# Weight chunks subtracted in quarters, and attention weights scaled by one operation with two per-row factors

## The chip, the cores and the metric

The kernel runs on one core of one Trainium2 chip. The metric is the time of one execution in microseconds on the device. The core has five engines that run side by side, each through its own queue in order: TensorE (PE in the profile, PEld for its weight loads), VectorE (DVE), ScalarE (ACT), GpSimd (POOL) and SyncE (SP), which here issues the DMAs. Tiles lie in SBUF, and matmuls write into eight PSUM banks.

## The reference, cut to what matters

One layer of a decoder trunk over 1024 tokens of width 1024, in float32: a normalisation, one input projection, a convolution group, a group of sparse attention with three gated branches, an output projection with a residual add, then a second normalisation and a SwiGLU feed-forward part.

```python
def hybrid_layer(x, ...):
    h = rms_norm(x, attn_norm)
    z = h @ w_in
...
    conv_out = conv_mixer(a_conv, conv_w, conv_b, conv_ln_g, conv_ln_b)
...
    gates = jax.nn.sigmoid(g).reshape(b, t, N_KV_HEADS, Q_PER_KV, N_BRANCH)
    nsa_out = nsa_attention(q, kc, vc, ks, vs, kw, vw, gates)
    x = x + concatenate([conv_out, nsa_out]) @ w_out
    h = rms_norm(x, ffn_norm)
    gate, up = jnp.split(h @ w_gate_up, 2, axis=-1)
    return x + (jax.nn.silu(gate) * up) @ w_down
```

Inside the attention, each branch is a masked softmax `p = exp(s - m) / max(sum, 1e-30)`, multiplied with the values, and the branch outputs are added with the gates as weights: `gb[..., 1:2] * o_s + gb[..., 2:3] * o_w`. So a row of `exp(s - m)` has two factors that are constant along the row: the gate and the inverse of the row's sum.

## The kernel before, in words

Matmuls are made as three products each. A float32 matrix is split into a high part, its rounding to the matmul's format, and a low part, the rest; high x high, low x high and high x low are summed in PSUM. For activations the split is the helper `split` (ACT copies L194, DVE subtracts L195). For weights it is `load_w`: SP loads a chunk of 128 x 1024 numbers (1096 for the value weights) into `w_raw`, ACT rounds it into `w_hi` (L189), and POOL subtracts into `w_lo` (L190). There are 168 such chunks on POOL, and eight more, for the compression weights, that DVE subtracts. Two buffers hold raw chunks and three hold each part; a `Feed` asks for chunks some places ahead. A second loader, `out_loads_k`, does the same with 16 chunks of 512 columns for the output projection of the second half (L887, L888).

The program has stages. In the first (until about 250 us) x is normalised and transposed, the compressed branch is made, the first half's rows are projected, and DVE runs the convolution: `conv_taps` adds 31 taps, each a `scalar_tensor_tensor` over 128 x 512 (L481), whose two tensor inputs both lie in SBUF. From about 250 us the function `attention` runs, woven by hand (`weave`, with costs and ratios) with a second stream that fills PE: first the second half's projections and the first half's output projection, from about 600 us passes of the feed-forward part for the first half (`ffn`, matmuls L991 and L1011). In the later attention part the taps of the second half run too (`slow`), now with factors that POOL copies into `c2` (L477, L478). From about 1000 us the second half's output projection and the rest of the feed-forward part follow.

An attention step is one of 64 pairs of a query tile and a branch, with three heads each. `scores` makes the scores on PE (L677 to L681); DVE adds the distance penalty and finds the minimum (L685); ACT takes the exponential with the row's sum in `l3` (L688). After the third head DVE bounds `l3` from below (L693), takes the reciprocal (L695) and multiplies it by the gates into `cf` (L696), all on 128 x 3 numbers. POOL then multiplies each head's row tile `pr` by its column of `cf`, spread along the row (L702): three operations of 128 to 1024 columns a step, 192 in all. `transposed` brings `pr` through PE (L708) and splits it, `product` multiplies with the values (L725, L726). Scores are asked for at least two steps ahead of their products, further where buffers and `LEAD` allow.

In `ffn`, ACT and DVE form `silu(gate) * up` in `af` (L998) and `split` turns it into `aw`; its subtraction (L195, `aw<-af,aw`) reads two SBUF tiles, while the other splits by DVE mostly read one PSUM and one SBUF tile.

The order of each engine's queue is not that of the source: the kernel is built with a scheduler that simulates the engines (`schedule_with_timeline_sim=True`) and places the instructions by that, except in the very last pass, where PE is kept in source order.

Of the kernel before, what the change touches and what calls it, by code (L numbers as in the profile page):

```python
# [11 lines left out]
F32 = mybir.dt.float32  # L12
F32R = mybir.dt.float32r
AF = mybir.ActivationFunctionType
ALU = mybir.AluOpType
# [3 lines left out]
P = 128  # L19
# [8 lines left out]
REP = HEADS // GROUPS  # L28
# [45 lines left out]
TICK = 5.0  # L74
SLOW0 = 36
PACE_B = 4
PRE_DVE = 0, 0
ACCS = "zs"
ACCS2 = "z"
ACCS3 = "z"  # L80
PACE_C = 0


@with_exitstack
def tile_hymba(ctx: ExitStack, tc, x, attn_norm, w_in, conv_w, conv_b, conv_ln_g, conv_ln_b,
# [3 lines left out]
    dve, act, pool, pe, sp = nc.vector, nc.scalar, nc.gpsimd, nc.tensor, nc.sync  # L89
# [12 lines left out]
    def bank(name, tag="z"):  # L102
        return ps.tile([P, 512], F32, tag=tag, name=name, bufs=BANKS[tag])
# [22 lines left out]
    gates = cp.tile([P, NT, 36], F32, name="gates")  # L126
# [51 lines left out]
    def load_w(parts, a, b, eng=pool):  # L178
        raw = wp.tile([P, WCH], F32, tag="raw", name="w_raw", bufs=2)
        hi = wp.tile([P, WCH], F32R, tag="whi", name="w_hi")  # L180
        lo = wp.tile([P, WCH], F32R, tag="wlo", name="w_lo")
        back = PACE_B if phase[0] == 0 else PACE_C
        if len(pace) >= back > 0:
            pool.tensor_copy(raw[:, 0:1], pace[-back][:, 0:1])
        n = a * b
        v = raw[:, :n].rearrange("p (k c) -> p k c", k=a)
        for c, src in parts:
            sp.dma_start(v[:, :, c:c + src.shape[-1]], src.rearrange("(k p) c -> p k c", p=P))
        act.copy(hi[:, :n], raw[:, :n])  # L189
        eng.tensor_sub(lo[:, :n], raw[:, :n], hi[:, :n].bitcast(F32))  # L190
        return (hi[:, :n].rearrange("p (k c) -> p k c", k=a), lo[:, :n].rearrange("p (k c) -> p k c", k=a))

    def split(hi, lo, src):
# [43 lines left out]
    def win_chunk(c0):  # L237
        return load_w([(0, w_in[0, :, c0:c0 + P])], KT, P)

    xts = []  # L240
    for t in range(NT):
# [4 lines left out]
        else:  # L246
            q_, tag = (p2, "xt") if t < 7 else (py, "y")
# [165 lines left out]
    def value_loads(c0, g0):  # L413
        return [lambda kh=kh: load_w([(0, w_in[0, kh * 512:(kh + 1) * 512, c0:c0 + 256]),
                                      (256, w_in[0, kh * 512:(kh + 1) * 512, C_G + g0:C_G + g0 + 18])], 4, 274)
                for kh in range(2)]
# [182 lines left out]
    def attention(p, bufs, extra, ratio):  # L599
# [4 lines left out]
        def size(st):  # L604
            i = st[2]
            return i + 1 if st[3] == 0 else min(i + 1, 5)
# [44 lines left out]
        def scores(st, r):  # L651
            part, g, i, br = st
            hf = i // 4
            if r == 0:
                load(st)
            nk = size(st)
            k0 = i + 1 - nk
            n = nk * P
            cut = {5: 384, 7: 384}.get(nk, 512)
            edges = [0, n] if n <= 512 else [0, cut, n]  # L660
            if r == 0:
                prs[st] = [p.tile([P, REP], F32, tag="l3", name="l3", bufs=26)]
            l3 = prs[st][0]
            q2, kk_ = q2s[g, i], kt[part, g, br]
            if hf:
                pr = p.tile([P, T], F32, tag="pr", name="pr", bufs=bufs["pr"])
            else:
                if br == 1:
                    both[g, i, r] = p.tile([P, T], F32, tag="pr", name="pr", bufs=bufs["pr"])
                pr = both[g, i, r][:, (1 - br) * 512:(2 - br) * 512]  # L670
            m = 3.0e38
            dur = 0.0
            for a, e in zip(edges, edges[1:]):
                s = bank("s", "s")
                sv = s[:, :e - a]
                kk = slice(k0 * P + a, k0 * P + e)
                pe.matmul(sv, q2[:, 0, r, :], kk_[:, 0, kk], start=True, stop=False)  # L677
                if br == 0 and hf:
                    pe.matmul(sv, q2[0:80, 1, r, :], kk_[0:80, 1, kk], start=False, stop=True)
                else:  # L680
                    pe.matmul(sv, q2[:, 0, r, :], kk_[:, 1, kk], start=False, stop=True)  # L681
                dur += 2 * max(0.107, (e - a) / 2400.0)
                mn = p.tile([P, 1], F32, tag="m", name="m", bufs=16)
                t0 = T if br and nk == 5 and a == 0 else T - n + a
                dve.tensor_tensor_reduce(pr[:, a:e], sv, base[:, t0:t0 + e - a], SLOPES[g * REP + r], m,  # L685
                                         ALU.add, ALU.min, mn)
                m = mn
            act.activation(pr[:, :n], pr[:, :n], AF.Exp, bias=m, scale=-1.0, accum_out=l3[:, r:r + 1])  # L688
            prs[st].append(pr)
            if r == REP - 1:  # L690
                pace.append(l3)
                cf = p.tile([P, REP], F32, tag="cf", name="cf", bufs=10)
                dve.tensor_scalar(l3, l3, 1e-30, None, op0=ALU.max)  # L693
                gv = gates[:, i, g * 9:(g + 1) * 9].rearrange("p (r b) -> p r b", b=3)[:, :, 1 + br]
                dve.reciprocal(l3, l3)  # L695
                dve.tensor_tensor(cf, gv, l3, op=ALU.mult)  # L696
                for r2 in range(REP):
                    x_ = prs[st][1 + r2][:, :n]
                    if r2 < PRE_DVE[part]:
                        dve.tensor_scalar(x_, x_, cf[:, r2:r2 + 1], None, op0=ALU.mult)  # L700
                    else:
                        pool.tensor_tensor(x_, x_, cf[:, r2:r2 + 1].to_broadcast([P, n]), op=ALU.mult)  # L702
            return dur

        def transposed(st, kk):
# [45 lines left out]
        for n in range(-1, len(steps)):  # L751
            phase[:] = [steps[max(n, 0)][0], n]
            want, ahead = n + 2, 0.0
            while want < len(steps) and fits(n, want) and ahead < LEAD:
                ahead += cost[want - 1]
                want += 1
            want = min(want, len(steps))
            todo = [(st, r) for st in steps[asked:want] for r in range(REP)]
            asked = max(asked, want)
            if n < 0:  # L760
                load_pct(steps[0])
            elif steps[n][3] and n + 2 < len(steps):
                load_pct(steps[n + 2])
            ts = range(size(steps[n])) if n >= 0 else []
            m = max(len(ts), 1)
            total, given = len(todo), 0
            for k in range(m):
                if n >= 0:
                    ph, pl = transposed(steps[n], k)
                    yield 0.33  # L770
                    pend.append((steps[n], k, ph, pl))
                    if len(pend) > LAG:
                        yield product(*pend.pop(0))
                while given * m < total * (k + 1):
                    yield scores(*todo[given])
                    given += 1
            for fn in extra.get(n, ()):
                d = fn()
                if d:
                    yield d  # L780
# [100 lines left out]
    def out_loads_k(p):  # L881
        def load(kt, ch):
            raw = p.tile([P, 512], F32, tag="oraw", name="o_raw")
            hi = p.tile([P, 512], F32R, tag="ohi", name="o_hi", bufs=2)
            lo = p.tile([P, 512], F32R, tag="olo", name="o_lo", bufs=2)
            sp.dma_start(raw, w_out[0, kt * P:(kt + 1) * P, ch * 512:(ch + 1) * 512])
            act.copy(hi, raw)  # L887
            pool.tensor_sub(lo, raw, hi.bitcast(F32))  # L888
            return hi, lo
        return [lambda kt=kq * 4 + k, ch=ch: load(kt, ch) for kq in range(2) for ch in range(2) for k in range(4)]  # L890

# [241 lines left out]
```

## Time and profile before

| | us |
|---|---|
| median of 3 runs | 1563.87 |
| lowest and highest | 1562.23, 1564.19 |
| profiled execution, its own time | 1562.75 |
| its span in the trace | 1561.0 |
| mean granted TensorE clock | 0.979 |

In the profile, a group's row gives line, engine, operation and tiles, then shapes and count, busy microseconds and mean nanoseconds of one, and last the idle time of the engine ahead of it with what ended it. A row of one line or tile gives shortest/median/longest nanoseconds. A row of the timeline gives start, length, engine and operation, with followers of one kind merged (x3). The chain of waits is followed back from the last instruction, at each step to what released it.

### The profile page before, as it was taken

To read this page: it belongs to the slowest core of one execution; us is meant where nothing else is said; L and a number is where in the kernel's file an instruction comes from. 1 tells how busy PE (TensorE), PEld (TensorE's weight loads), DVE (VectorE), ACT (ScalarE), POOL (GpSimd) and SP (SyncE) were. 2 spreads that over 40 slices of the span, in tenths; PEclk is the share of its full clock that TensorE was granted. 3 is DMA by queue.
4 is the path that set the end of the run, shared out by engine and by line. 5 is a ranking of instruction groups with operands and counts; after the bars stand their busy time and mean duration, and the time that the engine had idled before them with its cause. 6 is when DMAs were issued, how large, how long until landed. Compare 5 with 4: busy or idle time off the path is not lost.

```text
span 1561.0 us, 21253 instructions
## 1 busy us (share of the span) xinstructions
PE 1475.6 (95%) x7271; PEld 1227.0 (79%) x7271; DVE 920.2 (59%) x1998; ACT 717.0 (46%) x1464; POOL 771.2 (49%) x618
## 2 busy tenths in 40 slices
PE   6998999899889989989999999999999999999997
PEld 5877978787668768878888887778788888888876
DVE  7596563778777677887778877332532432222333
ACT  6334564668576566555665564322311222222223
POOL 6253253767556546656656655444322243444443
PEclk9999999999989999999999999999999999999999
DMA  6254566566476463234245222742121233233332
GB/s 195 79 144 133 169 192 213 170 179 189 132 255 173 118 142 87 70 100 117 68 119 135 60 61 74 242 145 88 48 75 54 89 114 94 81 107 96 94 95 81
DMA packets 224265, 190.44 MB, mean 122 GB/s; under 512 B 15400, under 2 KB 193420, under 8 KB 224156
## 3 DMA queue, kind: packets, MB, share of 16 engines
q1 hardware_dynamic: 224156, 189.07, 41.3%
q8 instruction: 58, 0.95, 0.3%
q14 instruction: 51, 0.42, 0.1%
HBM read 155.27 MB, written 33.75 MB: 121 GB/s over the span
## 4 chain that ended last, share of the span: by engine, by line
PE 69%; DVE 12%; ACT 6%; DMA 5%; issue 4%; POOL 2%; SPq 1%; POOLq 0%; DVEq 0%; ACTq 0%
PE gu L991 28%; PE dn L1011 14%; PE pt L708 4%; DVE cacc L481 4%; PE vo L427 3%; PE wo L934 3%; PE wo L952 3%; PE o L726 2%; PE o L725 2%; PE s L677 2%; PE zc L314 2%; DMA w_raw<-in_w_in_dram 2%; DMA mix<-mix_d 2%; PE zo L314 2%; ACT w_hi L189 1%
## 5 line engine op out<-in xcount | busy, mean ns | idle before, releaser
L190 POOL TENSOR_TENSOR w_lo<-w_raw,w_hi 128x1024 fp32r<-128x1024 f32 (+1 forms) x168 | 419.2, 2502 | 436.8 <-ACT w_hi L189 413.6
L991 PE MATMUL gu<-h,w_hi 128*128 128x512 f32 x1408 | 455.0, 396 | 0.6 <-DVE x L1016 0.6
L189 ACT CAST w_hi<-w_raw 128x1024 fp32r<-128x1024 f32 (+1 forms) x176 | 183.9, 1051 | 353.8 <-PE gu L991 180.8
L991 PEld LDWEIGHTS gu<-h,w_hi 128*128 128x128 f32 x1408 | 263.3, 188 | 57.6 <-DVE x L1016 1.1
L991 PE MATMUL gu<-h,w_lo 128*128 128x512 f32 x704 | 278.3, 395 | 0.0
L1011 PE MATMUL dn<-w_hi,aw 128*128 128x512 f32 x704 | 235.8, 399 | 12.7 <-DVE aw L195 6.0
L702 POOL TENSOR_TENSOR pr<-pr,cf 128x640 f32<-128x640 f32 (+5 forms) x192 | 214.4, 1144 | 66.3 <-DVE cf L696 51.9
L688 ACT ACTIVATE pr<-pr,m 128x640 f32<-128x640 f32 (+5 forms) x192 | 141.5, 738 | 121.4 <-DVE m L685 116.6
L998 DVE TENSOR_TENSOR af<-gu,af 128x512 f32<-128x512 f32 x44 | 30.3, 688 | 246.0 <-PE gu L991 184.9
L1011 PEld LDWEIGHTS dn<-w_hi,aw 128*128 128x128 f32 x704 | 131.4, 188 | 48.8 <-DVE aw L195 8.9
L195 DVE TENSOR_TENSOR pl<-pt,ph 128x384 fp32r<-128x384 f32 x264 | 140.5, 550 | 42.6 <-ACT ph L194 41.0
L1016 DVE TENSOR_TENSOR x<-dn,x 128x512 f32<-128x512 f32 x176 | 114.8, 684 | 76.0 <-PE dn L1011 75.8
L991 PEld LDWEIGHTS gu<-h,w_lo 128*128 128x128 f32 x704 | 132.3, 188 | 28.9
L194 ACT CAST ph<-pt 128x384 fp32r<-128x384 f32 x264 | 118.2, 478 | 72.3 <-PE pt L708 55.8
L708 PE MATMUL pt<-ident,pr 128*128 128x128 f32 x792 | 141.5, 279 | 6.7 <-DVE pl L195 5.7
L1011 PE MATMUL dn<-w_lo,aw 128*128 128x512 f32 x352 | 138.8, 394 | 0.0
L708 PEld LDWEIGHTS pt<-ident,pr 128*128 128x128 f32 x792 | 103.8, 143 | 24.9 <-DVE pl L195 4.0
L685 DVE CUSTOM_DVE_ANT_0 pr<-s,base 128x384 f32<-128x384 f32 (+3 forms) x192 | 101.3, 533 | 27.1 <-PE s L681 15.6
L677 PE MATMUL s<-kt,q 128*128 128x384 f32 (+3 forms) x288 | 104.2, 363 | 11.5 <-DVE m L685 8.0
L314 PE MATMUL zo<-h,w_hi 128*128 128x512 f32 x320 | 107.0, 407 | 5.4 <-ACT w_hi L189 2.8
L725 PE MATMUL o<-ph,vt 128*128 128x384 f32 x264 | 101.9, 386 | 4.0 <-ACT ph L194 3.8
L726 PE MATMUL o<-pl,vt 128*128 128x384 f32 x264 | 94.2, 357 | 2.4 <-DVE pl L195 2.4
(208 smaller groups left out, 2454.0 us busy)
## 6 DMA issues: line engine op xcount, KB each, us to landing
w_raw<-in_w_gate_up_dram SPq DMA_DIRECT2D x80, 512.0 KB, 3.8
w_raw<-in_w_in_dram SPq DMA_DIRECT2D x40, 512.0 KB, 4.2
w_raw<-in_w_down_dram SPq DMA_DIRECT2D x40, 512.0 KB, 3.3
mix<-mix_d SPq DMA_DIRECT2D x8, 1024.0 KB, 7.8
q<-q_d SPq DMA_DIRECT2D x80, 96.0 KB, 2.7
qc<-q_d SPq DMA_DIRECT2D x32, 192.0 KB, 3.6
pc_d<-pct SPq DMA_DIRECT2D x16, 384.0 KB, 3.1
pct<-pc_d SPq DMA_DIRECT2D x32, 192.0 KB, 3.8
```

The source lines that it names most:

```text
L189: act.copy(hi[:, :n], raw[:, :n])
L190: eng.tensor_sub(lo[:, :n], raw[:, :n], hi[:, :n].bitcast(F32))
L195: dve.tensor_sub(lo, src, hi.bitcast(F32))
L314: pe.matmul(o, a[:, k, :], b[hf][k // 4][:, k % 4, :], start=n == 0, stop=n == 3 * KT - 1)
L677: pe.matmul(sv, q2[:, 0, r, :], kk_[:, 0, kk], start=True, stop=False)
L688: act.activation(pr[:, :n], pr[:, :n], AF.Exp, bias=m, scale=-1.0, accum_out=l3[:, r:r + 1])
L702: pool.tensor_tensor(x_, x_, cf[:, r2:r2 + 1].to_broadcast([P, n]), op=ALU.mult)
L708: pe.transpose(pt[:, r * P:(r + 1) * P], prs[st][1 + r][:, kk * P:(kk + 1) * P], ident)
L725: pe.matmul(o[:, :384], v, ph, start=False, stop=False)
L726: pe.matmul(o[:, :384], v, pl, start=False, stop=last)
L991: pe.matmul(o, w[:, k, :], h2[si][h][k // 4][:, k % 4, :], start=n == 0, stop=n == 3 * KT - 1)
L1011: pe.matmul(o, aws[si][:, a, k, t * P:(t + 1) * P], b[:, 0, ch * 512:(ch + 1) * 512], start=n == 0, stop=n == 5)
```

## The change

POOL's subtraction of a weight chunk becomes four subtractions of a quarter of the columns each, and the one of the second loader two halves. DVE no longer forms `cf`, and POOL multiplies each row tile by two per-row factors in one tensor-scalar operation: the inverse sum in `l3` and the gate, read from `gates` itself. The constant `PRE_DVE`, which was zero for both parts, goes with the branch that used it.

```diff
-PRE_DVE = 0, 0
...
+PIECES = 4
...
@@ load_w
         act.copy(hi[:, :n], raw[:, :n])
-        eng.tensor_sub(lo[:, :n], raw[:, :n], hi[:, :n].bitcast(F32))
+        step = n // PIECES if eng is pool else n
+        for c in range(0, n, step):
+            q = slice(c, c + step)
+            eng.tensor_sub(lo[:, q], raw[:, q], hi[:, q].bitcast(F32))
...
@@ scores
                 pace.append(l3)
-                cf = p.tile([P, REP], F32, tag="cf", name="cf", bufs=10)
                 dve.tensor_scalar(l3, l3, 1e-30, None, op0=ALU.max)
-                gv = gates[:, i, g * 9:(g + 1) * 9].rearrange("p (r b) -> p r b", b=3)[:, :, 1 + br]
                 dve.reciprocal(l3, l3)
-                dve.tensor_tensor(cf, gv, l3, op=ALU.mult)
+
                 for r2 in range(REP):
                     x_ = prs[st][1 + r2][:, :n]
-                    if r2 < PRE_DVE[part]:
-                        dve.tensor_scalar(x_, x_, cf[:, r2:r2 + 1], None, op0=ALU.mult)
-                    else:
-                        pool.tensor_tensor(x_, x_, cf[:, r2:r2 + 1].to_broadcast([P, n]), op=ALU.mult)
+                    c = g * 9 + r2 * 3 + 1 + br
+                    pool.tensor_scalar(x_, x_, l3[:, r2:r2 + 1], gates[:, i, c:c + 1], op0=ALU.mult, op1=ALU.mult)
...
@@ out_loads_k
             act.copy(hi, raw)
-            pool.tensor_sub(lo, raw, hi.bitcast(F32))
+            for c in (0, 256):
+                q = slice(c, c + 256)
+                pool.tensor_sub(lo[:, q], raw[:, q], hi[:, q].bitcast(F32))
             return hi, lo
```

In the built program the instructions are otherwise the same, with two more loads of an ACT table; the scheduler moves many of them by some places. POOL's four quarters of a chunk stand mostly in a row, and PE waits for them one by one: 390 products with a `w_lo` wait for POOL, where 119 did.

## The prediction

> **What bounds the kernel now.** I read the page first, then the busy time by stage, then the chain of waits.
>
> ```profile
> span 1561.0 us, 21253 instructions
> PE 1475.6 (95%) x7271; PEld 1227.0 (79%) x7271; DVE 920.2 (59%) x1998; ACT 717.0 (46%) x1464; POOL 771.2 (49%) x618
> ...
> PE 69%; DVE 12%; ACT 6%; DMA 5%; issue 4%; POOL 2%; SPq 1%; POOLq 0%; DVEq 0%; ACTq 0%
> ```
> ```profile
> 0.00:250.00 250.00, 222.01 (x1170) 190.28 (x1171) 165.61 (x305) 121.56 (x274) 107.74 (x110) 0.96 0.54 161
> 250.00:600.00 350.00, 317.10 (x1721) 269.51 (x1720) 258.75 (x800) 223.78 (x582) 207.74 (x221) 0.95 0.57 163
> 600.00:1000.00 400.00, 387.88 (x2009) 324.81 (x2008) 310.42 (x662) 232.61 (x417) 238.14 (x183) 1.00 0.36 100
> 1000.00:1500.00 500.00, 496.69 (x2157) 401.44 (x2156) 161.97 (x198) 120.81 (x160) 192.44 (x92) 1.00 0.30 94
> ...
> 1184.41 44.55 PE gu L991 x192
> ```
> The columns are the stretch, its length, busy PE, weight loads, DVE, ACT, POOL, then clock, DMA share and GB/s; the last row, of the chain in order of time, is 192 matmuls without a break, 0.232 us apart. TensorE sets the time. From 1000 to 1500 us it is busy for 496.7 of 500 us, so nothing done to POOL or DVE can pay there. What can be won lies before 1000 us, where PE idles 28, 33 and 12 us (a busy PE there isn't at its peak either), and on the chain the largest share that isn't PE is DVE's, 12%. POOL is idle half the time and holds 2% of the chain. Its own speed matters little, but what it does to DVE matters:
>
> ```profile
> L195 DVE TENSOR_TENSOR aw<-af,aw x44: 677/2210/2877, 611.6 to 1542.4; 128x512 fp32r<-128x512 f32 x44
> ...
> L481 DVE SCALAR_TENSOR_TENSOR cacc<-y,c,cacc x58: 735/1134/2860, 589.9 to 955.9; 128x512 f32<-128x512 f32 x58
> ...
> 85.78 2.82 POOL L190 TENSOR_TENSOR w_lo<-w_raw,w_hi 128x1024 fp32r<-128x1024 f32 x1
> ...
> 83.61 2.76 DVE L481 SCALAR_TENSOR_TENSOR cacc<-y,cols,cacc 128x512 f32<-128x512 f32 x1
> 86.29 0.14 DVE L372 COPY bc<-h 128x1 f32<-128x1 f32 x1
> ```
> The first two rows give shortest/median/longest ns of DVE operations with both inputs in SBUF. An `aw` takes 677 ns at best but 2210 in the median; the excess never passes 2.2 us, about one POOL subtraction. The last rows show it once: a tap that needs 735 ns stands for 2.76 us, until POOL's subtraction ends at 85.8 us. The next subtraction, begun at 85.78, takes 2.82 us. Such an operation and a POOL instruction exclude each other, and a waiting DVE operation gets in between two POOL instructions.
>
> **Quartering, from 600 to 1000 us.**
>
> ```profile
> 600.00:1000.00 400.00, 25.42 (x14) 1.00 0.36 100
> ...
> 600.00:1000.00 400.00, 70.95 (x56) 1.00 0.36 100
> ...
> 600.00:1000.00 400.00, 0.00 (x0) 99.45 (x41) 1.00 0.36 100
> ...
> 600.00:1000.00 400.00, 111.07 (x71) 1.00 0.36 100
> ...
> by line: PE gu L991 26.9%; PE dn L1011 15.9%; PE pt L708 8.7%; issue 5.4%; DVE cacc L481 5.1%; PE o L726 4.9%; PE o L725 4.7%; PE s L677 4.1%; DVE aw L195 3.8%; DVE pr L685 2.7%; DVE pl L195 2.4%; PE s L679 2.3%; ACT w_hi L189 1.7%; PE s L6
> ...
> PE dn L1011 <- DVE aw L195: 6.0, 5, 2.9
> ```
> The four windows are `aw`, the taps L481, POOL's subtractions L190 (DVE's zero ahead of them) and its scalings L702; a number in brackets is a count. An `aw` averages 25.42/14 = 1.82 us, 63% of it over the 0.677 floor; a tap 70.95/56 = 1.27 us, 42% over 0.735. The chain holds 3.8% of 400 = 15.2 us of `aw` and 5.1% = 20.4 us of taps, so the blocked part on it is 0.63 x 15.2 + 0.42 x 20.4 = 18.1 us.
>
> How much goes? A random arrival waits half the POOL instruction that it meets: (99.45 x 1.21 + 111.07 x 0.78)/400 = 0.52 us now. Prices of the new pieces:
>
> ```profile
> L190 POOL TENSOR_TENSOR w_lo<-w_raw,w_hi 128x1024 fp32r<-128x1024 f32 x160 | 398.7, 2499 | 415.8 <-ACT w_hi L189 392.7 <-DVE cm L538 9.7 <-issue 8.9
> L702 POOL TENSOR_TENSOR pr<-pr,cf 128x640 f32<-128x640 f32 x60 | 82.6, 1404 | 16.9 <-DVE cf L696 13.5 <-PE s L677 3.2
> L888 POOL TENSOR_TENSOR o_lo<-o_raw,o_hi 128x512 fp32r<-128x512 f32 x16 | 20.7, 1293 | 42.4 <-ACT o_hi L887 42.4
> ...
> L281 POOL TENSOR_SCALAR cb<-cb 128x512 f32<-128x512 f32 x1 | 2.1, 2066 | 0.1
> ...
> L302 POOL TENSOR_SCALAR_AFFINE_SELECT base<-base 128x1024 f32<-128x1024 f32 x1 | 1.0, 1034 | 0.0
> L282 POOL TENSOR_SCALAR_AFFINE_SELECT cb<-cb 128x512 f32<-128x512 f32 x1 | 0.6, 648 | 0.0
> ```
> A subtraction of 512 costs 1293 ns and one of 1024 costs 2499, so the fixed part is 2 x 1293 - 2499 = 87 ns and a quarter is 87 + 2412/4 = 690 ns. The new scaling has no good row. Its nearest kin by pattern, one input and one output, are the selects: 648 ns at 512 and 1034 at 1024, which puts 640 columns at 745 ns, 0.53 of the 1404 now. The one tensor-scalar row takes 2066 ns for 512, which scaled is 2.58 us, 1.84 times. But that row stood against DVE:
>
> ```profile
> 23.93 2.07 POOL L281 TENSOR_SCALAR cb<-cb 128x512 f32<-128x512 f32 x1
> ...
> 23.36 4.09 DVE L203 SCALAR_TENSOR_TENSOR xt<-xt,rs,grow 128x1024 f32<-128x1024 f32 x3
> ...
> L203 DVE SCALAR_TENSOR_TENSOR rows<-x,rs,rows x12: 1270/1284/3447, 569.1 to 1246.0; 128x1024 f32<-128x1024 f32 x12
> ```
> Three two-input operations of 1.27 us each at best fill 23.36 to 27.45 us with 0.28 us lost. Had POOL needed the port for 2 us, they would have lost 2. Most of that span was waiting, so I take 0.53. [...]
>
> With quarters of 0.69 us and scalings of 0.83 (0.53 x 1.56) the mean wait becomes (41 x 4 x 0.69 x 0.345 + 71 x 0.83 x 0.415)/400 = 0.16 us: 69% goes, 12.5 of the 18.1 us. A second chain lies behind, so not all is time. PE itself waited for `aw` 6.0 us, of which 69% is 4.1. Between 4.1 and 12.5 I take **-8 us**.
>
> **The attention stage, 250 to 600 us.**
>
> ```profile
> L693 DVE TENSOR_SCALAR l<-l x64: 146/169/2335, 254.2 to 942.0; 128x3 f32<-128x3 f32 x64
> ...
> L693 DVE TENSOR_SCALAR l<-l 128x3 f32<-128x3 f32 x64 | 28.0, 438 | 21.1 <-ACT pr L688 20.8
> ...
> L696 DVE TENSOR_TENSOR cf<-gates,l 128x3 f32<-128x3 f32 x64 | 17.0, 266 | 1.2
> ```
> The product `cf` (L696) goes, 17.0 us of DVE. L693 averages 0.438 us over a floor of 0.146, so 64 x 0.29 = 18.6 us are blocked there. With the product that is 36 us at most, over both attention parts. A step's three scalings also end 3 x 0.66 = 2 us earlier. But scores are asked for steps ahead, and what covers the chain from scores to scaling now keeps covering it. Between 0 and 0.69 x 18.6 + 17.0 = 30 us I take a tenth, **-3 us**.
>
> **The first stage, and what the change adds.**
>
> ```profile
> L481 DVE SCALAR_TENSOR_TENSOR cacc<-y,cols,cacc 128x512 f32<-128x512 f32 x62 | 59.4, 994 | 0.6
> ...
> by line: DVE cacc L481 14.6%; PE zc L314 12.5%; PE vo L427 9.6%; issue 7.2%; POOL w_lo L190 5.1%; ACT w_hi L189 3.5%; DMA w_raw<-in_w_in_dram 3.4%; ACT cs L544 3.2%; PE tp L210 2.5%; DVE w_lo L190 2.5%; DMA xt<-in_x_dram 2.4%; DMA w_raw<-in
> ...
> 113.77 4.05 DVE L481 SCALAR_TENSOR_TENSOR cacc<-y,cols,cacc 128x512 f32<-128x512 f32 x6
> ...
> 114.86 5.23 POOL L190 TENSOR_TENSOR w_lo<-w_raw,w_hi 128x1024 fp32r<-128x1024 f32 x1 [5.54 <-ACT w_hi L189]
> ```
> Taps hold 14.6% of 250 = 36.5 us of the chain, 26% of it over 735 ns, so up to 0.69 x 9.5 = 6.6 us could go. Against it, the port works the other way too: at 114.86 us a subtraction sat behind six taps in a row and took 5.23 us instead of 2.4. A chunk needs one gap in such a run now and four after. I set this stage at **0**, between -6.6 and the price of the third rival.
>
> POOL pays 3 x 87 = 261 ns more per chunk, 168 chunks, 44 us. It hides under POOL's 51% idle; at the end a chunk is wanted once in 24 matmuls (5.6 us at 0.232 us each). Were the cover gone, the 5.1% of 250 us with L190 on the chain, about five chunks, would pay 1.3 us. The product by a low part can now start at its first quarter, up to 1.8 us sooner for those five, 9 us at most. I take **0** for both. Extra PE waits on met semaphores and local shuffles of the built order I take at nothing: PE at 496.7 of 500 us covers them late, and early they are inside the range.
>
> **Sum.** -8 - 3 + 0 = -11 us on the profiled execution's own 1562.75 us (its span and 1.75 us around it): 1551.8. The median shown, 1563.87, lies 1.1 us above it, so 1553 us.
>
> **Rivals.** *Hidden anyway.* DVE's lost time sits beside waits for DMA and ACT (11% of the chain), and what is won is waited again before the saturated stage. Then 1561 to 1567. For it: only 6.0 us of PE idle names `aw`. Against: 18 us of blocking on the chain itself. *It doesn't do what it says*: DVE finds no gap between quarters in a row. The same time, about 1565; the tap let in at 85.8 speaks against it. *DVE starves POOL* in runs of taps before 130 us: each further quarter sits through a run, 5.23 - 2.4 = 2.8 us, three times a chunk, 8.5 us. It decides if three of the first stage's chunks are late enough to hold PE: +25 us against the 11, so about 1577. For it: 114.86. Against: the taps too are finite, and the projections' own DVE work, which waits for PE, breaks their runs. [...] *The slow scaling*: at 1.84 times, POOL has 0.84 x 111 = 93 us more in the 400 us from 600 on, 331 of 400 busy, and a step's three scalings end 3.5 us later; if a third of 64 steps show it, +75 us, 1638.
>
> **How the numbers follow.** Forecast 0.57 (1536 to 1560, the bounds of the terms), hidden 0.08, not as said 0.03, starving 0.22, slow scaling 0.10. The range 1535 to 1577 holds the first four but for tails and leaves the last out. No change is within 0.2%, 3.1 us, what a measurement of this kernel can tell. Faster 0.57, same 0.11, slower 0.32.
>
> **What would show it.** In the new profile: `aw`'s median below 1.3 us; taps' means near 0.8 us; scalings of 640 near 0.75 us; quarters near 0.69 us; L693 near 0.2 us; DVE's share of the chain under 12%; 1000 to 1500 us unchanged. It is wrong if subtractions in the first stage take 3 us a quarter with PE waiting for L190, or if scalings take over 1.4 us.

## The result, and the profile after

The changed kernel takes 1524.01 us (median of 4 runs, 1521.04 to 1528.14), against 1563.05 us (4 runs, 1559.24 to 1564.19) of the kernel before: ratio 0.976, 95% interval 0.9736 to 0.9784. It is 39 us faster. The forecast was 11 us, and its range ended at 1535: the direction was right, the size was not.

The page of the changed kernel first, then its busy time by stage (columns as before).

```profile
span 1522.3 us, 21776 instructions
...
PE 1457.7 (96%) x7271; PEld 1219.8 (80%) x7271; DVE 813.1 (53%) x1934; ACT 718.9 (47%) x1466; POOL 806.2 (53%) x1138
...
PE 72%; DVE 9%; DMA 6%; ACT 5%; POOL 4%; issue 3%; SPq 0%; POOLq 0%; DVEq 0%; ACTq 0%
```
```profile
0.00:250.00 250.00, 221.94 (x1170) 189.44 (x1171) 155.38 (x305) 123.97 (x277) 127.35 (x189) 0.97 0.56 163
250.00:600.00 350.00, 330.28 (x1850) 282.85 (x1849) 247.24 (x790) 239.03 (x609) 215.20 (x314) 0.98 0.59 169
600.00:1000.00 400.00, 394.37 (x2044) 334.40 (x2044) 260.26 (x615) 225.80 (x402) 226.11 (x318) 1.00 0.38 108
1000.00:1500.00 500.00, 497.31 (x2156) 402.77 (x2155) 138.07 (x202) 121.76 (x160) 230.44 (x313) 1.00 0.29 90
```

PE does the same 7271 matmuls. In the first 250 us it does exactly as many of them as before (1170), from 1000 to 1500 us as many to one (2157 before). The gain lies in between: 129 matmuls more from 250 to 600 us (1721 before), 35 more from 600 to 1000 (2009 before). In the second stage there are two effects: PE is busy for 13 us more, and the granted clock is 0.98 instead of 0.95. The middle of that stage, before and after:

```profile
400.00:600.00 200.00, 176.93 (x913) 147.89 (x912) 150.03 (x435) 126.90 (x298) 113.67 (x105) 0.92 0.54 153
```
```profile
400.00:600.00 200.00, 187.97 (x1024) 158.37 (x1023) 148.76 (x441) 138.08 (x318) 120.86 (x163) 0.98 0.56 163
```

Here 11 us of idle time went. In these 200 us nine stretches of 3.41 us stood at half the clock, after the change two; in both traces 128x512 matmuls start 427 ns apart in the median at half the clock and 232 at full. So the seven are worth an estimated 11 us more (7 x 3.41 x (1 - 232/427)).

The rows that the prediction named, after the change: `aw`; the taps of both halves (now L484) with shortest/median/longest; then POOL's groups and L693 (now L695), each with its mean behind the comma.

```profile
L198 DVE TENSOR_TENSOR aw<-af,aw x44: 680/816/1301, 581.5 to 1503.7; 128x512 fp32r<-128x512 f32 x44
```
```profile
L484 DVE SCALAR_TENSOR_TENSOR cacc<-y,cols,cacc x62: 732/752/1310, 62.9 to 928.3; 128x512 f32<-128x512 f32 x62
L484 DVE SCALAR_TENSOR_TENSOR cacc<-y,c,cacc x58: 735/751/1596, 576.8 to 925.5; 128x512 f32<-128x512 f32 x58
```
```profile
L193 POOL TENSOR_TENSOR w_lo<-w_raw,w_hi 128x256 fp32r<-128x256 f32 x640 | 492.6, 803 | 368.5 <-ACT w_hi L189 358.2 <-PE zo L317 3.8 <-DVE bt L595 2.3
L701 POOL TENSOR_SCALAR pr<-pr,l,gates 128x640 f32<-128x640 f32 x60 | 52.8, 892 | 67.6 <-DVE l L696 65.3 <-ACT ou L728 2.4
...
L701 POOL TENSOR_SCALAR pr<-pr,l,gates 128x1024 f32<-128x1024 f32 x12 | 14.3, 1203 | 7.8 <-PE o L725 6.4 <-DVE l L696 1.4
...
L701 POOL TENSOR_SCALAR pr<-pr,l,gates 128x128 f32<-128x128 f32 x24 | 10.4, 448 | 10.6 <-DVE l L696 10.6
```
```profile
L695 DVE TENSOR_SCALAR l<-l 128x3 f32<-128x3 f32 x64 | 16.8, 263 | 23.3 <-ACT pr L691 23.0
```

All of them moved as forecast: `aw` from 2210 to 816 ns in the median, the second half's taps to a median of 751 ns, a scaling of 640 columns from 1404 to 892 ns, L693 from 438 to 263 ns. So the operations did what was said. What they are worth was said wrongly, and the experiments are about that.

The table below shows how far a kernel's PE is ahead (negative) of the kernel before when it has done the same matmul work, counted in columns streamed, at the moments at which the kernel before stood at 250, 400, 600, 800, 1010 and 1500 us. It is worked out from all matmul records of one profiled execution each. idle_pool takes the time of the kernel before and still stands at -9.3 at 600 us, so a lead of some 10 us at one moment can be order alone.

| kernel | 250 | 400 | 600 | 800 | 1010 | 1500 |
|---|---|---|---|---|---|---|
| after | 0.0 | -4.4 | -24.9 | -32.0 | -39.2 | -38.0 |
| quarters_only | -1.3 | -7.3 | -15.9 | -18.7 | -25.3 | -27.8 |
| quarters_rest | 0.4 | -7.5 | -16.9 | -17.1 | -5.0 | -6.8 |
| quarters_ffn | -1.8 | 0.9 | -2.7 | -12.3 | -19.1 | -19.4 |
| scale_only | 0.0 | 0.8 | -11.6 | -16.2 | -20.7 | -24.2 |
| scale_with_cf | -0.8 | 7.6 | 19.5 | 17.6 | 15.8 | 13.2 |
| heads_reversed | -0.4 | 4.0 | -4.7 | -5.8 | -6.1 | -7.1 |
| idle_pool | -0.5 | -2.4 | -9.3 | -10.8 | -4.2 | -1.7 |

### The profile page after: what moved, and what is told of

It reads as the page before. It is cut to its first block, busy times and chain, and to the rows that moved or that the text cites. A ratio compares the mean times of both kernels' runs of the same rounds, so it can differ in the third digit from the quotient of the medians.

```text
span 1522.3 us, 21776 instructions
## 1 busy us (share of the span) xinstructions
PE 1457.7 (96%) x7271; PEld 1219.8 (80%) x7271; DVE 813.1 (53%) x1934; ACT 718.9 (47%) x1466; POOL 806.2 (53%) x1138
## 4 chain that ended last, share of the span: by engine, by line
PE 72%; DVE 9%; DMA 6%; ACT 5%; POOL 4%; issue 3%; SPq 0%; POOLq 0%; DVEq 0%; ACTq 0%
PE gu L992 30%; PE dn L1012 14%; PE pt L707 4%; PE zo L317 4%; PE wo L935 3%; DVE cacc L484 3%; PE o L725 2%; PE vo L430 2%; PE o L724 2%; PE s L680 2%; PE zc L317 2%; PE wo L953 2%; DMA w_raw<-in_w_in_dram 2%; POOL pr L701 1%; POOL w_lo L193 1%
## 5 line engine op out<-in xcount | busy, mean ns | idle before, releaser
L193 POOL TENSOR_TENSOR w_lo<-w_raw,w_hi 128x256 fp32r<-128x256 f32 (+1 forms) x672 | 517.5, 803 | 394.5 <-ACT w_hi L189 378.4
L701 POOL TENSOR_SCALAR pr<-pr,l,gates 128x640 f32<-128x640 f32 (+5 forms) x192 | 150.5, 798 | 124.5 <-DVE l L696 106.1
L707 PE MATMUL pt<-ident,pr 128*128 128x128 f32 x792 | 136.9, 277 | 2.1 <-DVE pl L198 1.1
L707 PEld LDWEIGHTS pt<-ident,pr 128*128 128x128 f32 x792 | 102.9, 142 | 18.6 <-issue 2.3
L680 PE MATMUL s<-kt,q 128*128 128x384 f32 (+3 forms) x288 | 101.0, 354 | 5.3 <-DVE m L688 4.7
```

The lines of the kernel that those rows point to most:

```text
L193: eng.tensor_sub(lo[:, q], raw[:, q], hi[:, q].bitcast(F32))
L701: pool.tensor_scalar(x_, x_, l3[:, r2:r2 + 1], gates[:, i, c:c + 1], op0=ALU.mult, op1=ALU.mult)
L707: pe.transpose(pt[:, r * P:(r + 1) * P], prs[st][1 + r][:, kk * P:(kk + 1) * P], ident)
```

## The experiments

Each time is a median, each ratio stands against the kernel before, timed beside it, with its 95% interval. Microseconds won or lost are the ratio times 1561.

### The two halves of the change alone

quarters_only is the kernel before with this:

```diff
-        eng.tensor_sub(lo[:, :n], raw[:, :n], hi[:, :n].bitcast(F32))
+        step = n // PIECES if eng is pool else n
+        for c in range(0, n, step):
+            q = slice(c, c + step)
+            eng.tensor_sub(lo[:, q], raw[:, q], hi[:, q].bitcast(F32))
...
-            pool.tensor_sub(lo, raw, hi.bitcast(F32))
+            for c in (0, 256):
+                q = slice(c, c + 256)
+                pool.tensor_sub(lo[:, q], raw[:, q], hi[:, q].bitcast(F32))
```

> The kernel before with the quarters (and halves of the second loader) alone; the product cf and the two-input scaling by it stay. Port theory (DVE's two-input operations wait for whole POOL subtractions): most of the gain is here, 1563 down to 1535 to 1545, and the aw median falls from 2.2 to under 1.3 us. Latency theory (the attention step from exponential to transpose is what got shorter): little of it, 1555 to 1563, with aw falling just as much. Order theory (the scheduler's other order made the gain): no saying, and it need not add up with the next run.

scale_only is the changed kernel with whole chunks, so the new scaling alone.

> The changed kernel with whole-chunk subtractions again: the one-input scaling by two factors and no product cf. Port theory: a third of the gain at most, 1548 to 1558, since scalings of 0.88 us instead of 1.40 hold the port for less. Latency theory: most of the gain, 1528 to 1540, taken between 250 and 600 us. Order theory: the two runs' gains do not add up to the 39 us of both.

Measured: quarters_only 1532.46 us, 0.9815 (0.9786 to 0.9845), 27 to 29 us won; scale_only 1537.58 us, 0.9854 (0.9824 to 0.9884), 23 us won. Each alone is worth at least twice the whole forecast. Their sum, about 52 us, is more than the 38 of both, so they share some of what they win.

### What in the scaling pays: one operation, the product, or the length

In the kernel before, POOL's multiplication by a spread column becomes a tensor-scalar operation. DVE still forms `cf`, so neither DVE's instructions nor the reads of the gates change. scale_with_cf:

```diff
-                        pool.tensor_tensor(x_, x_, cf[:, r2:r2 + 1].to_broadcast([P, n]), op=ALU.mult)
+                        pool.tensor_scalar(x_, x_, cf[:, r2:r2 + 1], None, op0=ALU.mult)
```

> The kernel before with one edit: POOL scales by a tensor-scalar operation with the one factor cf, which DVE still forms. If the shorter POOL operation is what counts, it gives what the two-factor scaling gives, within 3 us. If the removed product counts (17 us of DVE, on every step's path), it lies 5 us or more above that run.

quarters_scale_with_cf is the same with chunks in quarters.

> Quarters and the one-factor scaling by cf: the change without the removal of DVE's product. If the product costs nothing, 1524 within 3 us; if it is on the path of 64 steps at some 0.16 us each, 1530 to 1535. Order theory: it differs from 1524 by more than 5 us in either direction with no cause in the operations.

Measured: scale_with_cf 1577.24 us, 1.0096 (1.006 to 1.0133), 15 to 18 us *lost*; quarters_scale_with_cf 1556.43 us, 0.9973 (0.9959 to 0.9987). The loss in the first was forecast by neither theory. POOL's groups in scale_with_cf say why:

```profile
L702 POOL TENSOR_SCALAR pr<-pr,cf 128x640 f32<-128x640 f32 x60 | 116.0, 1949 | 15.3 <-DVE cf L696 11.1 <-PE wo L934 3.8
L702 POOL TENSOR_SCALAR pr<-pr,cf 128x512 f32<-128x512 f32 x24 | 37.2, 1572 | 9.8 <-DVE cl L546 6.7 <-DVE cf L696 3.1
L702 POOL TENSOR_SCALAR pr<-pr,cf 128x1024 f32<-128x1024 f32 x12 | 36.1, 3025 | 1.7 <-DVE cf L696 1.7
...
L702 POOL TENSOR_SCALAR pr<-pr,cf 128x128 f32<-128x128 f32 x24 | 14.2, 607 | 6.5 <-DVE cf L696 5.3 <-ACT ph L194 1.2
```

With one factor, 640 columns take 1949 ns; with two factors, in the changed kernel, 892. The form that does less takes more than twice as long. So the next kernel, scale2_with_cf, gives that operation a second factor that does nothing:

```diff
-                        pool.tensor_tensor(x_, x_, cf[:, r2:r2 + 1].to_broadcast([P, n]), op=ALU.mult)
+                        pool.tensor_scalar(x_, x_, cf[:, r2:r2 + 1], 1.0, op0=ALU.mult, op1=ALU.mult)
```

> The kernel before with the scaling as a two-operation tensor-scalar, by cf and then by the constant 1.0; DVE's product cf stays. If the form with a second operation is what is fast, 640 columns take 0.88 us here too, against 1.95 us with one operation. Then against the scaling edit without cf (1537.6): if the shorter POOL operation gives that gain, 1535 to 1543; if the removed product gives it, 1553 to 1560.

quarters_scale2_with_cf is the same with quarters, which is the changed kernel with the product `cf` put back.

> The changed kernel, but with the product by the gates still formed by DVE and a scaling by that product and the constant 1.0. Without quarters this form gave 0.9878 and the form without the product 0.9854. If a step's product costs the same 4 to 5 us here: 1528 to 1530. If the quarters leave DVE free early enough to hide it: within 2 us of 1524.

Measured: scale2_with_cf 1542.8 us, 0.9878 (0.9853 to 0.9902), 19 us won; quarters_scale2_with_cf 1521.5 us, 0.9739 (0.9711 to 0.9768), 41 us won. The rows for 640 columns, the latter's first:

```profile
L706 POOL TENSOR_SCALAR pr<-pr,cf 128x640 f32<-128x640 f32 x60 | 57.1, 968 | 13.2 <-DVE cf L700 13.2
```
```profile
L702 POOL TENSOR_SCALAR pr<-pr,cf 128x640 f32<-128x640 f32 x60 | 55.3, 937 | 20.9 <-DVE cf L696 20.7
```

With whole chunks the product's removal is worth 0.9878 - 0.9854 = 0.0024, 4 us, and the intervals overlap. With quarters it is worth nothing that these runs can tell. The scaling's gain comes from POOL's shorter operation, nearly all of it.

The kernels with the one-factor form also tell *how* a shorter operation pays. Between 250 and 1010 us the DVE operations of scale_with_cf take 81 us more than the shortest of their kind (line, tiles and shape), those of the kernel before 114. So DVE is blocked *less* there, and the kernel is slower all the same. What is longer is the step: from the start of its first scaling to the end of its third, a step needs 3.35 us in the mean before, 4.89 in scale_with_cf, 2.37 after, 2.34 in scale2_with_cf (the last 32 steps alone 4.62, 6.56, 2.91 and 3.09). In the last 32 steps of the kernel before, 16 have their first transpose less than 1 us behind the end of the last scaling, and 15 of these ahead of it: PE begins with a head that is done while POOL scales the next. The median is 0.80 us, after the change 1.97 us. But PE hardly stands still for a scaling. From 250 to 1010 us the kernel before has this one wait of the kind, and scale_with_cf has none:

```profile
PE pt L708 <- POOL pr L702: 0.3, 1, 0.3
```

So the times show that the length of a step's scalings counts; by which of PE's waits it does is not shown.

### More POOL work that nothing waits for

If POOL's load mattered and not the step, extra POOL work would cost. idle_pool is the kernel before with 16 small writes to an unused tile behind each step's scalings, 1024 in all:

```diff
+                dm = p.tile([P, 32], F32, tag="dm", name="dm")
+                pool.tensor_copy(dm[:, :REP], l3)
+                for _ in range(16):
+                    pool.memset(dm, 0.0)
```

> The kernel before plus work for POOL that nothing waits for: a small copy of l3 and sixteen memsets of 32 columns after each step's scalings, about 1.5 us a step and 100 us in all, as much as the one-factor scaling added (which made 1560 into 1577). If POOL's time as such is what the scaling edit saved (its queue delays weight chunks and copies), 1570 to 1580. If the delay from exponential to transpose is what counts, within 5 us of 1560, as the memsets stand mostly behind the scalings.

Measured: 1559.88 us, 0.9989 (0.9973 to 1.0004). Its row for that work:

```profile
L706 POOL MEMSET dm<- 128x32 f32 x1024 | 127.4, 124 | 49.0
```

127 us of POOL's time cost nothing. A scaling that is 0.55 us longer, 192 times, some 100 us, cost 15 to 18 us. So it is not how full POOL is that counts, but the length of a step's scalings. The memsets do not hold DVE up either (the 16 taps and `aw` that begin under one lose 9 ns in the median), so this run tests POOL's load alone.

### Order alone

The scheduler moves thousands of places whatever is edited. heads_reversed changes nothing but the order in which a step's three scalings are issued, in the kernel before; after_heads_reversed does it in the changed one.

```diff
-                for r2 in range(REP):
+                for r2 in reversed(range(REP)):
```

> The kernel before, with the three heads' scalings issued last head first. No operation changes; the transposes wait for all three anyway. It moves as many places in the scheduler's order as the scaling edit did, so it shows what another order alone is worth. Order theory: 10 us or more off 1560 in either direction. If the two edits' gains belong to their operations: within 5 us of 1560.

> The changed kernel with the same reversal. Order theory: 10 us or more off 1524. Otherwise within 5 us of it.

Measured: 1555.19 us, 0.9953 (0.9933 to 0.9972), and 1524.31 us, 0.9753 (0.973 to 0.9777), as against 0.976. Another order moved the one kernel by 7 us and the other by nothing that shows. It is not quite order alone: with its first head scaled last, no step's transposes begin ahead of the third scaling's end, so "the transposes wait for all three anyway" does not hold for the kernel before. Differences below some 7 us between kernels of this study are therefore not read as causes.

### Where the quarters pay

quarters_ffn has quarters only for the feed-forward part's chunks, quarters_rest for all the others of `load_w`. A flag that the feed-forward loads set decides:

```diff
+        step = n // PIECES if eng is pool and ffn_now[0] else n
```

> The kernel before with quarters only for the 120 chunks of the feed-forward part. If their gain comes from DVE's aw and taps, which stand beside these chunks: 1538 to 1548. If it comes from the chunks of the projections, between 250 and 600 us: 1553 to 1560.

> Quarters for all chunks of load_w but those of the feed-forward part; all chunks in quarters gave 0.9815 (about -27 us), the feed-forward ones alone 0.9868 (about -21 us). If the two groups act each for itself: -6 us, near 1554. If what counts is that DVE is blocked less anywhere before 1000 us, the first stage's taps included: -10 to -15 us, 1545 to 1550. If the first stage has nothing to gain and the rest is noise of the order: 1557 to 1561.

Measured: quarters_ffn 1539.92 us, 0.9868 (0.9846 to 0.989), 21 us; quarters_rest 1551.97 us, 0.9936 (0.991 to 0.9961), 10 us. The table above shows where. quarters_ffn wins 16 us between 600 and 1010 us and little ahead of it. quarters_rest wins 17 us between 250 and 600 us, where the second half's projections run beside the attention, nothing ahead of 250, and then loses 12 of them again beside the chunks left whole; up to some 10 us of such a lead can be order, as idle_pool's shows.

### By which way: `aw`, or another

aw_psum, in the kernel before, leaves POOL alone and lets `silu(gate) * up` be written back to its PSUM bank, so that the subtraction which makes `aw` reads one SBUF tile only:

```diff
-                dve.tensor_tensor(af, gu[si][1], af, op=ALU.mult)
-                split(aws[si][:, 0, f2, :], aws[si][:, 1, f2, :], af)
+                dve.tensor_tensor(gu[si][1], gu[si][1], af, op=ALU.mult)
+                split(aws[si][:, 0, f2, :], aws[si][:, 1, f2, :], gu[si][1])
```

> The kernel before with silu(gate) * up written back into the PSUM bank of up, so that the split that makes aw reads one PSUM and one SBUF tile, and no POOL instruction changes. aw should fall from 1.8 us to 0.69. Port theory: 5 to 12 us are gained, less what the bank costs that is held some 1.3 us longer. If blocked aw does not matter: no gain, 1555 to 1565.

quarters_ffn_aw_psum has that and quarters for the feed-forward chunks.

> Quarters beside the feed-forward chunks together with the product silu(gate) x up written back into its PSUM bank, so that the subtraction that makes aw reads one SBUF tile only. Alone the quarters there gave 0.9868 (about -21 us) and the other edit 0.9972 (about -4 us). If the quarters win by unblocking aw, aw is unblocked already here and nothing is left for them: the two together give no more than the better one, and the price of the longer held bank (which must then be some 17 us) stays, 1550 to 1558. If the quarters win by another way than aw, the two add up: 1533 to 1538. Near 1540: aw's blocking is a small part, and the bank's price is small too.

Measured: aw_psum 1556.98 us, 0.9972 (0.9956 to 0.9988); quarters_ffn_aw_psum 1538.65 us, 0.9841 (0.9811 to 0.987). The `aw` row of aw_psum, and then PE's products with `aw` from 600 to 1010 us (the idle time ahead of them stands behind the second bar) in the kernel before, aw_psum, quarters_ffn and quarters_ffn_aw_psum:

```profile
L195 DVE TENSOR_TENSOR aw<-gu,aw x44: 675/691/692, 607.7 to 1541.3; 128x512 fp32r<-128x512 f32 x44
```
```profile
L1011 PE MATMUL dn<-w_hi,aw 128*128 128x512 f32 x224 | 81.3, 409 | 9.5 <-DVE aw L195 6.0 <-DVE af L998 2.2 <-DVE x L1016 1.0
```
```profile
L1011 PE MATMUL dn<-w_hi,aw 128*128 128x512 f32 x224 | 82.9, 420 | 10.5 <-ACT aw L194 5.9 <-DVE aw L195 3.7 <-DVE x L1016 0.7
```
```profile
L1021 PE MATMUL dn<-w_hi,aw 128*128 128x512 f32 x226 | 80.3, 402 | 2.0 <-DVE x L1026 1.4 <-DVE af L1008 0.3 <-ACT aw L199 0.2
```
```profile
L1021 PE MATMUL dn<-w_hi,aw 128*128 128x512 f32 x226 | 79.4, 401 | 1.1 <-ACT aw L199 1.1
```

In aw_psum every `aw` runs in 675 to 692 ns, none is blocked, and PE still idles 10.5 us ahead of its products: the wait has moved to the step ahead, ACT's rounding of `aw`. Quarters take the wait away whether `aw` was blocked (9.5 to 2.0 us) or not (10.5 to 1.1), and win the same: 0.9868 against before, and 0.9841/0.9972 = 0.9869 on top of aw_psum. So the 1.5 us that an `aw` lost to a subtraction is not what the quarters win; `aw` is late because what makes it is late. And this wait is only a part of the gain: it falls by 7.5 us in quarters_ffn, whose lead grows by 16 us in the same stretch.

### The early start, and the size of a piece

quarters_reversed issues a chunk's quarters from the last to the first. PE begins with the first, so its first low product waits for the whole chunk again, while DVE has its gaps.

```diff
+        for c in reversed(range(0, n, step)):
```

> The kernel before with quarters issued last quarter first, so that PE's first low product waits for the whole chunk again; what DVE sees of the port is as with the quarters alone (1532.5). Port theory: 1528 to 1538. If the early start at the first quarter gave the gain: 1550 to 1560. Both: in between.

Measured: 1540.16 us, 0.9847 (0.9813 to 0.9882), 24 us won; its interval overlaps that of quarters_only. By the medians the early start is worth 5 us; the intervals don't tell that from nothing, nor do they rule out more.

after_p2 and after_p8 are the changed kernel with halves and with eighths.

> The changed kernel with halves in place of quarters. By the waits for the port, a half of 1.29 us leaves twice a quarter's wait: 1528 to 1532 against 1524 with quarters and 1537.6 with whole chunks. If the number of pieces matters by their fixed cost on POOL: below 1524.

> The changed kernel with eighths. Whole chunks, halves and quarters gave 0.9854, 0.9807 and 0.976. If the length of one piece sets what a waiting DVE operation loses, the mean wait falls by another half of what quarters leave: 1518 to 1522. If the fixed price of a piece (a quarter took 803 ns in the mean, not 625) or the growing number of gaps that runs of taps fill takes over: 1524 to 1535.

Measured: 1529.91 us, 0.9807 (0.978 to 0.9834), and 1523.54 us, 0.9756 (0.9721 to 0.979). Whole, half, quarter, eighth give 0.9854, 0.9807, 0.976, 0.9756. Beyond quarters nothing comes. An eighth is dear:

```profile
L193 POOL TENSOR_TENSOR w_lo<-w_raw,w_hi 128x128 fp32r<-128x128 f32 x1280 | 589.8, 500 | 328.2 <-ACT w_hi L189 327.4 <-POOL oh L732 0.2
```

Two of them take 1000 ns, a quarter 803, so some 197 ns are fixed in each, waits among them. No version tried beats the changed kernel by more than the intervals hold.

## Why the prediction was wrong in size and right in sign

**The bound: right.** TensorE sets the time, nothing is won from 1000 to 1500 us (496.7 us busy before, 497.3 after; the table's lead moves by 1.2), and what is won lies in the stages that the prediction named.

**The attention stage, "I take a tenth, -3 us": this term failed.** The reason given was that what covers the chain from scores to scaling "now keeps covering it". It does not. By 600 us the changed kernel is 25 us ahead, and scale_only is ahead by 12 there and by 24 at the end. Three kernels with DVE's work on a step unchanged show it by size: a step's scalings done 1.0 us sooner in the mean won 19 us (scale2_with_cf, 2.34 against 3.35 us), 1.5 us later lost 15 to 18 (scale_with_cf, 4.89; the loss is all there by 600 us), while 2 us of POOL work behind the scalings of each step cost nothing (idle_pool). Over 64 steps that is an estimated 0.15 to 0.3 us of time for each microsecond of a step, so a part of it stays covered. The bound that I kept, 30 us, held the answer, but by luck, as it was set up on the wrong quantity: it counted DVE's blocked and removed work (18.6 and 17.0 us), and the product's 17.0 us turned out to be worth some 4 us by the medians, within the intervals, and nothing that shows beside quarters.

**The quarters, "between 4.1 and 12.5 I take -8 us": too small, and in the wrong bounds twice.** The stage was wrong: the prediction costed them from 600 us on only, and quarters_rest is 17 us ahead at 600, more than the 10 that order alone is seen to give, in a stage where the prediction's only term for quarters was L693's blocked time. And the carriers were wrong: the blocked part of `aw` and taps on the chain (18.1 us) was to be the most that could go. quarters_ffn wins 16 to 21 us, and it does so with `aw` unblocked beforehand as well. The operations did lose less, 816 ns against 2210, just as worked out, but their own excess didn't bound the gain: a part of what quarters took away, 7.5 of the 16 us, was PE's wait ahead of `dn`, which aw_psum shows to be one for the whole chain that makes `aw`. Nor were the taps with `c` blocked less by quarters alone: their excess over 735 ns was 30 us before, 36 in quarters_only, 20 in scale_only and 6.5 after the change. Before, 32 of the 58 begin under a scaling and lose 21 of the 30 us there; each edit leaves standing what the other takes away.

**The clock: left out.** I read PE's idle time as the loss. From 400 to 600 us the granted clock was 0.92 before and 0.98 after, worth an estimated 11 us beside the 11 of idle time. The two hang together. In the traces of all 18 kernels the granted clock is 1.00 or 0.50, and changes in steps of 3.41 us. Three such stretches of the kernel before, one in which PE idled and the two behind it (columns as before, busy PE first, the clock behind POOL):

```profile
567.50:570.91 3.41, 0.44 (x4) 0.44 (x5) 1.84 (x2) 1.35 (x4) 1.83 (x1) 1.00 1.03 252
570.91:574.32 3.41, 3.41 (x13) 2.63 (x11) 3.41 (x10) 2.81 (x5) 0.55 (x1) 0.50 1.16 252
574.32:577.73 3.41, 3.18 (x23) 2.66 (x22) 3.41 (x7) 2.88 (x6) 0.00 (x0) 1.00 0.16 63
```

Over these traces, from 250 to 1010 us, all 38 stretches at full clock in which PE was busy for less than 0.4 of the time were followed by one at half the clock, and none of the 3495 in which it was busy for 0.8 or more. The kernel before has 12 at half the clock there, the changed kernel 4, each of them behind one in which PE was busy for 0.62 of the time or less. By this an estimated 12 us of the 39 (8 x 3.41 x (1 - 232/427)) are a price of idle time on top of the idle time itself, and the prediction had no term for it.

**The first stage, 0: right.** Lead at 250 us: 0.0. With eighths it was 10 us, and the end came no sooner. **The early start and POOL's fixed cost, 0:** the start is some 5 us by the medians, within the intervals. The fixed cost was mis-sized (87 ns forecast; 803 - 2412/4 = 200 ns measured, waits among it) and hides all the same: POOL is busy for 806 us of 1522.

**Prices.** A quarter: 690 forecast, 803 measured in the mean. A scaling of 640: 745 forecast, 892 measured. The row that I set aside, 2066 ns for a tensor-scalar of 512, was mostly the operation's true price: scale_with_cf has 1572 ns in the mean of 24. The reason given ("Most of that span was waiting") was wrong: that DVE lost little beside the row (0.28 us) fits what the one-factor scalings show (last section), beside which 26 taps lose 6.1 us where 31.7 us of scaling were left. The forecast stood by luck, because with a second factor the operation is fast (1949 to 937 ns for 640 columns), and no row of the kernel before shows that.

**The rivals.** *Hidden anyway* and *not as said* fall with the 39 us. *DVE starves POOL*: the timeline of the changed kernel has a run of seven taps beside the four quarters of a chunk,

```profile
111.54 6.65 DVE L484 SCALAR_TENSOR_TENSOR cacc<-y,cols,cacc 128x512 f32<-128x512 f32 x7
...
112.27 4.72 POOL L193 TENSOR_TENSOR w_lo<-w_raw,w_hi 128x256 fp32r<-128x256 f32 x4 [3.85 <-PE zo L317]
```

and the four take 4.72 us, less than the 5.23 of one whole subtraction before, not four runs of taps; the taps take 0.95 us each. The two take turns. *The slow scaling* had the right mechanism at the wrong form: scale_with_cf is that kernel, with a price of 15 to 18 us and not 75. That a DVE operation with both inputs in SBUF and a POOL instruction exclude each other holds in the kernel before beside the subtractions (35 `aw` begin under one and lose 48.4 us where 52.8 us of subtraction were left) and beside the old scalings (32 taps, 21.0 of 27.0 us), but not beside this form (26 taps, 6.1 of 31.7 us). "The port" in the prediction and the expectations is a name for these waits, and the traces show the waits alone.

**What stays open.** By which way the quarters win beside the feed-forward chunks. It is not `aw`'s own blocked time, and the early start is some 5 us of it by the medians; PE's wait ahead of `dn` shows that DVE and ACT hand over `aw` sooner. Whether that comes from other operations of DVE that are blocked for shorter, or from another place that the scheduler gives them, no run here separates. Open too are by which of PE's waits a step's scalings count, how much of it is the other places that the scheduler gives to another form of operation, and why the gains of the two edits add up to 52 us alone and 39 together. A third buffer for raw chunks wasn't tried.

## What to carry to other kernels

Where a busy engine takes a result within a microsecond of its making, a shorter chain to that result can pay, however idle the engines of that chain are (here an estimated 0.15 to 0.3 us for each microsecond of a step); measure the gap between the last producer and the first consumer for each step before calling a latency covered. The blocked time in an operation's own rows is no upper bound for what shortening the blocker is worth: unblock the operation by itself once, and see whether the consumer's wait goes or only changes its name. Price an idle stretch with the clock that follows it (here 0.50 behind all 38 stretches in which PE was busy for less than 0.4). And edit the order alone once, to learn what a difference must exceed before it needs a cause.

## What the runs showed of the hardware

A GpSimd tensor-scalar operation on float32 with one per-row factor takes 2.70 ns per column in the mean, waits among it ((3025 - 607)/896; 2.50 by the fastest, (2843 - 599)/896), and with two factors 0.84 ((1203 - 448)/896); a multiplication by a spread column takes 1404 ns for 640. A second factor of 1.0 halves the one-factor form's time at 640 columns (1949 to 937 ns). So the one-factor form takes about three times as long per column as the two-factor form (2.70/0.84); why, no run shows.

The slow form is also the one beside which DVE was blocked less (81 us of excess against 114), and the traces show why. Before, 32 of the second half's taps begin while a scaling runs, and they wait for its end: they lose 21.0 us where 27.0 us of scaling were left, some 0.19 us less than that each. With two factors and `cf` (scale2_with_cf) 32 taps lose 13.6 of 19.4 us. Beside the one-factor form (scale_with_cf) 26 taps lose 6.1 us where 31.7 were left, and the 12 that begin more than 0.7 us behind its start lose at most 0.04 us each. So the length of a GpSimd operation alone does not say how long it keeps DVE out: the one-factor form, the longest, does so only in its first part.
